# S5 in a hybrid mixer block: one operation for both scan directions, and a sum moved from VectorE to TensorE

## The chip, the cores and the metric

The kernel runs on one core of a Trainium2 chip. The metric is the time of one execution on the device in microseconds, the median of several runs. The engines are called as in the profile: PE is TensorE (matmuls), DVE is VectorE, ACT is ScalarE, POOL is GpSimd, SP is SyncE, which only issues transfers. ACT and POOL also issue transfers from their own queues. Each engine and each queue works through its instructions in the order written by the scheduler of the program.

## The reference

Two layers of a latent generator at batch 1: 512 latent tokens and 256 context tokens of 1024 channels. In each layer one input projection is split into four mixers, their outputs are put together and projected, and a SwiGLU follows. The change is in the fourth mixer, S5: 16 groups of 16 channels, 64 complex states per group, two directions. Cut to what matters here:

```python
ab_re, ab_im, z_re, z_im = s5_discretize(a_re[r], a_im[r], log_dt[r])   # (G, P), direction r
bb_re = z_re[..., None] * b_re - z_im[..., None] * b_im
bb_im = z_re[..., None] * b_im + z_im[..., None] * b_re
bu = einsum('gpc,blgc->blgp', bb, u)                   # complex input of the state
h_t = ab * h_{t-1} + bu_t                              # complex scan over tokens
y = einsum('gcp,blgp->blgc', c_re, h_re) - einsum('gcp,blgp->blgc', c_im, h_im)
y_total = u * d_skip + y(forward) + y(reversed)        # then gelu and a gated projection
```

The latent scan starts from the last context state of its direction.

## The kernel before

Activations lie with channels on partitions and tokens along columns. Large projections are made in three matmuls each from a high and a low part of weight and activation (`whi`, `wlo`, `ahl`, `alol` and so on), the parts split by ACT and DVE from weights that SP loads into three rotating tiles `wst` (`weights`, `piece`). The adaLN modulation of layer 0 (`mod`) loads its weights `in_wm` through the same tiles and multiplies into the PSUM ring `md`, which has one buffer.

**S5.** The 768 tokens (context, latent) are cut into 96 steps of 8. Per state the scan over the 96 steps is real: the rotation by the angle of the eigenvalue is taken out first and put back behind. So there are four parts:

- `s5_prep` (L1445): powers 0 to 8 of each eigenvalue and their products with the input coefficient, for all groups and both directions (32 columns), with real parts and imaginary parts on the two halves of the partitions. They land in `S` (tile `early` for layer 0, `S5S` for layer 1) at `S_X`, `S_N`, `S_Y`, `S_M`. The columns are ordered direction first, then group.
- `rotations` (L1512): cosine and sine of 96 multiples of an angle, as the complex product of 16 fine and 6 coarse ones (`R`, `R2`), for two groups at a time (`NG = 2`): `cmul` makes six DVE operations on 192 columns (tiles `cst`, `s5tq`), and ACT's queue writes each block of two groups to DRAM (`s5r`). There are 8 blocks.
- `s5_mats` (L1560): for each block and direction the input matrix `W` (8 steps by 16 channels) and the output matrix `oe` (9 steps by 16 channels, in tile `s5M`), each from two products and a difference. PE transposes `W`, ACT copies the transpose into `s5M`, PE makes the kernel inside one step (`Kf`), and ACT's queue writes it to DRAM eight times shifted (`s5k`).
- `s5_block` (L1642): SP loads the rotations (`s5rot`), the matrix `KT` from `s5k` and the input `U`. PE makes the state's input twice (`pv`), DVE multiplies by cosine and sine and adds (`gt`, `g2`), four scans run over the steps (line 1686, tile `g`), DVE multiplies again by the cosine (`gt`) and, with the halves of the partitions exchanged, by the sine (`sg`, in the profile `s5sg`), and adds both. `s5_y` (L1702) sums `KT` times `U` and `oe` times `gt` in PSUM, ring `md`, and ACT's queue writes the result to DRAM (`s5y`). `s5_out` reads it back (`s5fu`, `s5fy`).

For layer 0 (`run=True`) matrices and blocks are made together, in the first 300 us, beside the input projections and the Hyena filters (`hw`, `fs`, `flo`, `fo`, `win`, `ftab`, `F0l`). For layer 1 `prepare` (L1761) makes tables and matrices during layer 0's SwiGLU, writes them to DRAM, and `s5` loads them.

**What sets the order.** The program gives each part a priority (a lower number first) and a scheduler writes one order per engine by it, by the dependences and by its own running estimate of when an instruction could start. Layer 0's norms and first projections have 10000, `rotations` 9000, Hyena's context filters 36000, S5 40000, Hyena's latent filters 45000; projection matmuls get 300000 more (`bulk`), so that they fill the gaps of PE. A tile with `bufs=2` has two buffers, and its next user waits for the one before last.

Of the kernel before, what the change touches and what calls it, by code (L numbers as in the profile page):

```python
# [106 lines left out]
class Kern:  # L107
# [1337 lines left out]
    def s5_prep(self, i, S, p):  # L1445
# [30 lines left out]
        for q, x in enumerate((c, s_)):  # L1476
            for r in range(2):
                self.act(self.r8[64 * r:64 * r + 64, i, q], x[64 * r:64 * r + 64, 16 * r:16 * r + 16])
        X, N = S[:, 0:9], S[:, 9:18]
# [30 lines left out]
        self.cmul(S[:, self.S_Y:self.S_M], S[:, self.S_M:self.S_END], X[:, 0:8], N[:, 0:8], bc(zr, 8), bc(zi, 8), T)  # L1510

    def rotations(self, i, p):  # L1512


        R = p.tile([128, 44, 16], F32, name="rot")
        T = p.tile([128, 8, 16], F32, name="rotT")
        w = p.tile([128, 3, 16], F32, name="rotw")
        c, s_, t = w[:, 0], w[:, 1], w[:, 2]
        self.ts(w[:, 0:2], self.r8[:, i], 1.0)
        for at, n in ((0, 16), (32, 6)):  # L1520
            C, S = R[:, at:at + n], R[:, at + n:at + 2 * n]
# [16 lines left out]
        rd = self.dr.tile([16 // self.NG, 128, 2 * self.NG * 96], F32, name=f"s5r{i}")  # L1538
        for b in range(16 // self.NG):
            gs = slice(self.NG * b, self.NG * (b + 1))  # L1540
            cst = p.tile([128, 2, self.NG, 6, 16], F32, tag="cst", name="cst", bufs=2)
            tq = p.tile([128, self.NG, 6, 16], F32, name="s5tq")

            def fine(j):
                return R2[:, 16 * j:16 * j + 16, gs].rearrange("p b g -> p g b")[:, :, None, :].to_broadcast(
                    [128, self.NG, 6, 16])

            def coarse(j):
                return R2[:, 32 + 6 * j:38 + 6 * j, gs].rearrange("p a g -> p g a")[:, :, :, None].to_broadcast(
                    [128, self.NG, 6, 16])  # L1550
            self.cmul(cst[:, 0], cst[:, 1], coarse(0), coarse(1), fine(0), fine(1), tq)
            nc = self.nc
            nc.scalar.dma_start(rd[b], cst)
        return rd
# [5 lines left out]
    def s5_mats(self, i, p, S=None, run=False):  # L1560
# [12 lines left out]
        sh = [128, NG, 8, 16]  # L1573
        for b, g0 in enumerate(range(0, 16, NG)):
            M = p.tile([128, self.O_END], F32, tag="s5M", name="s5M", bufs=2)
            BC = p.tile([128, 6, NG, 16], F32, tag="s5BC", name="s5BC", bufs=2)
# [3 lines left out]
            ws = {}  # L1580
            for r in range(2):
                lg = slice(16 * r + g0, 16 * r + g0 + NG)

                def pw(at, n, rev):
                    v = S[:, at:at + n, lg]
                    if rev:
                        v = v[:, ::-1]
                    return v.rearrange("p t g -> p g t")[:, :, :, None].to_broadcast([128, NG, n, 16])

                def bc(q, n):  # L1590
                    return BC[:, q][:, :, None, :].to_broadcast([128, NG, n, 16])
                br, bi, cr, ci = bc(0, 8), bc(1, 8), bc(2 + r, 9), bc(4 + r, 9)

                Wt = p.tile(sh, F32, tag=f"W{r}", name="W", bufs=1 if run else 2)
                tmp = p.tile([128, NG, 9, 16], F32, tag="s5tmp", name="s5tmp")
                self.mul(Wt, pw(self.S_Y, 8, r == 0), br)
                self.mul(tmp[:, :, :8], pw(self.S_M, 8, r == 0), bi)
                self.sub(Wt, Wt, tmp[:, :, :8])
                ws[r] = Wt
                self.mul(oe[:, r], pw(self.S_X, 9, r == 1), cr)  # L1600
                self.mul(tmp, pw(self.S_N, 9, r == 1), ci)
                self.sub(oe[:, r], oe[:, r], tmp)
            W4 = self.pst()
            for g in range(NG):
                for r in range(2):
                    q = 128 * (NG * r + g)
                    nc.tensor.transpose(W4[:, q:q + 128], ws[r][:, g].rearrange("p t c -> p (t c)"), self.ident)
# [34 lines left out]
    def s5_block(self, i, b, p, M, kd, rd):  # L1642
# [8 lines left out]
        rot = p.tile([128, 2, 2, NG * 96], F32, tag="s5rot", name="s5rot", bufs=2)  # L1651
        for h in range(2):
            nc.sync.dma_start(rot[64 * h:64 * h + 64], rd[b].rearrange("(r n) x -> n r x", r=2))
        ct, st = rot[:, :, 0], rot[:, :, 1]
# [19 lines left out]
        def fl(t):  # L1674
            return t.rearrange("p r g b -> p r (g b)")
        self.mul(fl(gt), pv[0][:, :nn].rearrange("p (r x) -> p r x", r=2), ct)
        self.mul(fl(g2), pv[1][:, :nn].rearrange("p (r x) -> p r x", r=2), st)
        self.add(gt, gt, g2)
        for g in range(NG):
            for r in range(2):  # L1680
                lg = 16 * r + g0 + g
# [6 lines left out]
        sg = p.tile([128, 2, NG, 96], F32, tag="sg", name="s5sg")  # L1688
        self.mul(fl(gt), fl(g2), ct)
        self.stt(fl(sg)[0:64], fl(g2)[64:128], -1.0, st[64:128], ALU.mult, ALU.mult)  # L1690
        self.mul(fl(sg)[64:128], fl(g2)[0:64], st[0:64])
        self.add(gt, gt, sg)
        if i == 0:
            self.s5_y(i, b, p, KT, U, gt, oe, c0)
            return

        with self.at(self.tc.cur_priority + self.LAG):
            self.s5_y(i, b, p, KT, U, gt, oe, c0)
# [3 lines left out]
    def s5_y(self, i, b, p, KT, U, gt, oe, c0):  # L1702
# [321 lines left out]
def layout(inputs):  # L2024
# [93 lines left out]
```

## Time and profile before

| | us |
|---|---|
| median of three runs (1887.65 to 1890.61) | 1889.87 |
| the profiled execution | 1895.85 |
| its span, first to last instruction | 1894.1 |
| PE busy | 1761.3 |
| DVE busy | 1369.3 |
| ACT busy | 771.1 |
| POOL busy | 209.6 |

[...] Busy times are sums of what the profiler recorded for an engine's instructions, without double counting; the ends of matmuls are modelled. The span is divided between the engines very unevenly, so the stretches count more than the totals.

### The profile page before, as it was taken

To read this page: it belongs to the slowest core of one execution; us is meant where nothing else is said; L and a number is where in the kernel's file an instruction comes from. 1 tells how busy PE (TensorE), PEld (TensorE's weight loads), DVE (VectorE), ACT (ScalarE), POOL (GpSimd) and SP (SyncE) were. 2 spreads that over 40 slices of the span, in tenths; PEclk is the share of its full clock that TensorE was granted. 3 is DMA by queue.
4 is the path that set the end of the run, shared out by engine and by line. 5 is a ranking of instruction groups with operands and counts; after the bars stand their busy time and mean duration, and the time that the engine had idled before them with its cause. 6 is when DMAs were issued, how large, how long until landed. Compare 5 with 4: busy or idle time off the path is not lost.

```text
span 1894.1 us, 30868 instructions
## 1 busy us (share of the span) xinstructions
PE 1761.3 (93%) x11512; PEld 1539.6 (81%) x11512; DVE 1369.3 (72%) x3169; ACT 771.1 (41%) x1515; POOL 209.6 (11%) x273
## 2 busy tenths in 40 slices
PE   3789878898899999999999999999898889999997
PEld 1678767686789988888888899988776889899997
DVE  8788764677758899686675425689667797777776
ACT  4364234555326323321133223624575374344442
POOL 0201121223002000011123100201200010000000
PEclk9899979998899999999999999999999889999998
DMA  6657688765622335666654621665564323233331
GB/s 233 183 141 189 150 174 233 234 203 171 186 78 90 112 117 151 202 197 211 222 147 117 178 69 47 186 210 171 154 192 141 95 72 110 98 104 98 104 108 57
DMA packets 193098, 280.99 MB, mean 148 GB/s; under 512 B 51745, under 2 KB 127837, under 8 KB 192436
## 3 DMA queue, kind: packets, MB, share of 16 engines
q1 hardware_dynamic: 107188, 166.20, 29.0%
q10 hardware_dynamic: 55920, 64.72, 11.3%
q0 software_dynamic: 29840, 48.09, 9.4%
q8 instruction: 91, 1.49, 0.3%
q14 instruction: 59, 0.48, 0.1%
HBM read 235.00 MB, written 43.96 MB: 147 GB/s over the span
## 4 chain that ended last, share of the span: by engine, by line
PE 55%; DVE 12%; DMA 11%; issue 5%; ACT 4%; POOL 1%; ACTq 0%; SPq 0%; DVEq 0%; POOLq 0%
PE ps_mm L126 20%; PE ps_xb L126 12%; PE ps_xa L126 8%; PE ps_mm L487 6%; DMA mvw<-in_wmt_dram 5%; PE ps_md L126 4%; PE ps_xb L487 3%; PE ps_xa L487 1%; ACT L155 1%; DVE wlo L134 1%; DVE mvo L364 1%; DMA wst<-in_wi_dram 1%; DVE xl L152 1%; ACT E L155 1%; DMA wst<-in_wo_dram 1%
## 5 line engine op out<-in xcount | busy, mean ns | idle before, releaser
L155 ACT ACTIVATE whi<-wst 128x1024 fp32r<-128x1024 f32 (+3 forms) x206 | 179.8, 903 | 294.9 <-PE ps_mm L126 105.4
L134 DVE TENSOR_TENSOR wlo<-wst,whi 128x1024 fp32r<-128x1024 f32 (+3 forms) x206 | 213.1, 1050 | 71.0 <-ACT whi L155 69.9
L126 PE MATMUL ps_mm<-alol,whi 128*128 128x512 f32 (+1 forms) x528 | 199.5, 379 | 0.4 <-POOL alol L134 0.4
L126 PE MATMUL ps_mm<-ahl,whi 128*128 128x512 f32 (+1 forms) x528 | 197.6, 380 | 2.3 <-DVE BC L152 2.0
L126 PE MATMUL ps_mm<-ahl,wlo 128*128 128x512 f32 (+1 forms) x528 | 198.8, 377 | 0.0
L364 DVE SCALAR_TENSOR_TENSOR mvo<-mvw,crow 128x1024 f32<-128x1024 f32 x80 | 97.8, 1222 | 42.0 <-DMA mvw<-in_wmt_dram 40.7
L126 PE MATMUL ps_mm<-h,whi 128*128 128x512 f32 (+1 forms) x440 | 121.5, 358 | 2.4 <-DVE h L134 2.0
L126 PE MATMUL ps_mm<-ahc,whi 128*128 128x256 f32 x368 | 106.8, 294 | 12.3 <-ACT whi L155 8.3
L126 PEld LDWEIGHTS ps_mm<-ahl,whi 128*128 128x128 f32 x528 | 100.2, 192 | 19.9 <-issue 3.7
L126 PEld LDWEIGHTS ps_mm<-alol,whi 128*128 128x128 f32 x528 | 100.6, 190 | 19.3 <-issue 3.0
L126 PEld LDWEIGHTS ps_mm<-ahl,wlo 128*128 128x128 f32 x528 | 100.5, 190 | 16.8 <-issue 0.8
L126 PE MATMUL ps_mm<-aloc,whi 128*128 128x256 f32 x368 | 107.2, 292 | 1.6 <-DVE aloc L134 1.6
L126 PE MATMUL ps_mm<-ahc,wlo 128*128 128x256 f32 x368 | 106.1, 290 | 0.3 <-DVE wlo L134 0.3
L126 PE MATMUL ps_xb<-ahl,whi 128*128 128x512 f32 (+1 forms) x256 | 91.3, 361 | 5.6 <-ACT ahl L155 5.4
L126 PE MATMUL ps_xb<-alol,whi 128*128 128x512 f32 (+1 forms) x256 | 91.3, 359 | 0.5 <-DVE alol L134 0.3
L126 PE MATMUL ps_xb<-ahl,wlo 128*128 128x512 f32 (+1 forms) x256 | 90.8, 355 | 0.0
L126 PEld LDWEIGHTS ps_mm<-h,whi 128*128 128x128 f32 x440 | 75.7, 189 | 12.9 <-DVE h L134 2.5
L126 PEld LDWEIGHTS ps_mm<-ahc,whi 128*128 128x128 f32 x368 | 71.7, 197 | 15.8 <-ACT whi L155 8.5
L155 ACT ACTIVATE h<-sg 128x512 fp32r<-128x512 f32 (+1 forms) x70 | 37.3, 537 | 110.6 <-DVE sg L134 110.5
L126 PE MATMUL ps_xb<-h,whi 128*128 128x256 f32 x432 | 81.5, 284 | 0.0
L126 PE MATMUL ps_mm<-h,wlo 128*128 128x512 f32 (+1 forms) x220 | 78.9, 359 | 0.0
L155 ACT ACT_TABLE_LOAD x55 | 70.6, 1283 | 20.4 <-DMA vec<-in_vec_dram 3.6
(645 smaller groups left out, 5204.0 us busy)
## 6 DMA issues: line engine op xcount, KB each, us to landing
wst<-in_wu_dram SPq DMA_DIRECT2D x88, 512.0 KB
mvw<-in_wmt_dram POOLq DMA_DIRECT2D x56, 512.0 KB, 3.8
wst<-in_wi_dram SPq DMA_DIRECT2D x42, 512.0 KB
wst<-in_wm_dram SPq DMA_DIRECT2D x40, 512.0 KB
wst<-in_wd_dram SPq DMA_DIRECT2D x24, 384.0 KB
ftab<-in_c_ftL_dram POOLq DMA_DIRECT2D x32, 256.0 KB, 5.4
wst<-in_wd_dram SPq DMA_DIRECT2D x32, 256.0 KB
s5rot<-s5r SPq DMA_DIRECT2D x32, 192.0 KB
```

Source lines behind the costliest of these rows:

```text
L126: return self.nc.tensor.matmul(out, lhsT, rhs, start=start, stop=stop)
L134: return (eng or self.nc.vector).tensor_tensor(out, a, b, op=op)
L152: return self.nc.vector.scalar_tensor_tensor(out, a, s, b, op0=op0, op1=op1)
L155: return self.nc.scalar.activation(out, in_, func, bias=bias, scale=scale)
L364: self.nc.vector.scalar_tensor_tensor(o, st, 1.0, crow[:, q], op0=ALU.mult, op1=ALU.mult, accum_out=mv[:, c, q:q + 1])
L487: self.nc.tensor.matmul(ps, w[:, k], x[k], start=first and k + q == 0, stop=k + q == 5, skip_group_check=not first)
```

## The change

1. **Columns.** The 32 columns of the tables are ordered block, direction, group instead of direction, group; the host lays out `s5a` and `s5bc` so. A block's two directions lie side by side.
2. **Reversal once.** `s5_prep` makes the powers in a tile `F` (`s5F`), and eight ACT copies bring them to `S`, with the steps turned round for the direction that needs it. Before, each use read them turned round.
3. **Matrices.** `s5_mats` makes `W` and `oe` for both directions in one operation: six on 512 or 576 columns instead of twelve on 256 or 288.
4. **Rotations.** The fine table holds, side by side, (cos, sin) in one tile and (-sin, cos) in another; a table block is coarse cosine times the first plus coarse sine times the second: three operations on 384 columns. In DRAM and in `s5rot`, runs of 16 cosines and 16 sines alternate. ACT makes the four tiles in twelve copies.
5. **Layer 0 only.** ACT makes a second output matrix `os` from `oe`, with the partition halves exchanged and one of them negated, in a wider `s5M` (1920 columns instead of 1344; before the copies that part holds the temporary of `s5_mats`). The sine product `sg` is taken without exchange, in one operation, and is not added to `gt`; `s5_y` multiplies `gt` by `oe` and `sg` by `os` and sums in PSUM. `sg` has two buffers. Layer 1 keeps the old form.

```diff
-        self.cmul(S[:, self.S_Y:self.S_M], S[:, self.S_M:self.S_END], X[:, 0:8], N[:, 0:8], bc(zr, 8), bc(zi, 8), T)
+        self.cmul(F[:, self.S_Y:self.S_M], F[:, self.S_M:self.S_END], X[:, 0:8], N[:, 0:8], bc(zr, 8), bc(zi, 8), T)
+        for at, n, rev in ((self.S_X, 9, 1), (self.S_N, 9, 1), (self.S_Y, 8, 0), (self.S_M, 8, 0)):
+            for r in range(2):
+                t = F[:, at:at + n]
+                self.act(self.by_dir(S[:, at:at + n], r), self.by_dir(t[:, ::-1] if r == rev else t, r))
...
-        R2 = p.tile([128, 44, 16], F32, name="rot2")
-        self.act(R2[0:64], R[0:64])
-        for at, n in ((0, 16), (16, 16), (32, 6), (38, 6)):
-            self.act(R2[64:128, at:at + n], R[64:128, at:at + n][:, ::-1])
+        fine = [p.tile([128, 16, 2, 16], F32, name=f"rotf{j}") for j in range(2)]
+        coarse = [p.tile([128, 16, 6], F32, name=f"rotc{j}") for j in range(2)]
...
+            for j in range(2):
+                self.act(fine[j][hs, :, j], rows(0, 16))
+                self.act(fine[j][hs, :, 1 - j], rows(16, 16), scale=-1.0 if j else 1.0)
+                self.act(coarse[j][hs], rows(32 + 6 * j, 6))
...
-            self.cmul(cst[:, 0], cst[:, 1], coarse(0), coarse(1), fine(0), fine(1), tq)
+            for j, t in enumerate((cst, tq)):
+                self.mul(t, coarse[j][:, gs][:, :, :, None].to_broadcast(sh),
+                         fine[j][:, gs].rearrange("p g q b -> p g (q b)")[:, :, None, :].to_broadcast(sh))
+            self.add(cst, cst, tq)
...
-                self.mul(Wt, pw(self.S_Y, 8, r == 0), br)
-                self.mul(tmp[:, :, :8], pw(self.S_M, 8, r == 0), bi)
-                self.sub(Wt, Wt, tmp[:, :, :8])
-                ws[r] = Wt
-                self.mul(oe[:, r], pw(self.S_X, 9, r == 1), cr)
-                self.mul(tmp, pw(self.S_N, 9, r == 1), ci)
-                self.sub(oe[:, r], oe[:, r], tmp)
+            self.mul(Wt, pw(self.S_Y, 8), bc(0, 8))
+            self.mul(tmp[:, :, :8], pw(self.S_M, 8), bc(1, 8))
+            self.sub(Wt, Wt, tmp[:, :, :8])
+            self.mul(oe, pw(self.S_X, 9), bc(2, 9))
+            self.mul(tmp, pw(self.S_N, 9), bc(3, 9))
+            self.sub(oe, oe, tmp)
+            if run:
+
+                oe, os = [M[:, c:c + self.O_END - self.O_OE] for c in (self.O_OE, self.O_END)]
+                self.act(os[0:64], oe[64:128])
+                self.act(os[64:128], oe[0:64], scale=-1.0)
...
         self.mul(fl(gt), fl(g2), ct)
-        self.stt(fl(sg)[0:64], fl(g2)[64:128], -1.0, st[64:128], ALU.mult, ALU.mult)
-        self.mul(fl(sg)[64:128], fl(g2)[0:64], st[0:64])
-        self.add(gt, gt, sg)
         if i == 0:
-            self.s5_y(i, b, p, KT, U, gt, oe, c0)
+            self.mul(fl(sg), fl(g2), st)
+        else:
+            self.stt(fl(sg)[0:64], fl(g2)[64:128], -1.0, st[64:128], ALU.mult, ALU.mult)
+            self.mul(fl(sg)[64:128], fl(g2)[0:64], st[0:64])
+            self.add(gt, gt, sg)
...
+            for q, (oe, x) in enumerate(parts):
+                O = [oe[:, r, g, 1 - r:9 - r].rearrange("p t c -> p (t c)") for r in range(2)]
+                self.mm(o[:, f0:], O[0], x[:, 0, g, f0 - 1:95], False, False)
+                if need_c:
+                    self.mm(o[:, 0:31], O[1], x[:, 1, g, 65:96], False, False)
+                self.mm(o[:, 32:], O[1], x[:, 1, g, 1:65], False, q == len(parts) - 1)
```

**The order of the instructions.** It is written anew, and in layer 0's mixers it differs in most places; in layer 1 and in SwiGLU it is nearly the same. Three places count here. First DVE near layer 0's second last block (`g_2202` and `g_2172` are the tile of the four scans; `s5tmp`, `fo`, `hin` and `fr0l` belong to the next block's matrices, the Hyena filter and its convolution). Before:

```order
L134 TENSOR_TENSOR s5tmp<-early,s5BC 128x288
L134 TENSOR_TENSOR fo<-ps_xb,fe 128x256
L134 TENSOR_TENSOR fo<-fe,ps_xb 128x256
L1686 SCALAR_TENSOR_TENSOR g_2202<-dec_98,gt 128x96 x4
L134 TENSOR_TENSOR s5M<-s5M,s5tmp 128x288
L134 TENSOR_TENSOR gt<-g_2202,s5rot 128x384
L152 SCALAR_TENSOR_TENSOR s5sg<-g_2202,s5rot 64x384
L134 TENSOR_TENSOR s5sg<-g_2202,s5rot 64x384
L152 SCALAR_TENSOR_TENSOR hin<-ps_mm,vec,hin 128x511
L152 SCALAR_TENSOR_TENSOR hin<-ps_mm,vec,hin 128x255
L134 TENSOR_TENSOR gt<-gt,s5sg 128x384
```

And after the change:

```order
L134 TENSOR_TENSOR g_2172<-ps_xa,s5rot 128x384
L152 SCALAR_TENSOR_TENSOR frv<-ps_xb,vec 128x2
L149 TENSOR_SCALAR fr0l<-ps_xb 128x2
L134 TENSOR_TENSOR s5M<-early,s5BC 128x576
L134 TENSOR_TENSOR gt<-gt,g_2172 128x384
L757 RECIPROCAL fr0l<-fr0l 128x2
L134 TENSOR_TENSOR s5M<-s5M 128x576
L1705 SCALAR_TENSOR_TENSOR g_2172<-dec_98,gt 128x96 x4
L134 TENSOR_TENSOR gt<-g_2172,s5rot 128x384
L134 TENSOR_TENSOR s5sg<-g_2172,s5rot 128x384
```

The scans stand behind 545 rows of DVE before and 472 now; two half-height products and an addition have become one product.

Then PE at the last of layer 0's S5 blocks, where the output is summed (`ps_md`); `fh` and `w_1453` belong to the Hyena filter. Before:

```order
L126 MATMUL ps_xa<-s5U,s5M 128x96 x4
L126 MATMUL ps_xb<-w_1453,fh 128x256 x2
L126 MATMUL ps_md<-s5U,KT 128x96
L126 MATMUL ps_xb<-w_1453,fh 128x256 x2
L126 MATMUL ps_md<-gt,s5M 128x95
L126 MATMUL ps_md<-gt,s5M 128x31
L126 MATMUL ps_md<-gt,s5M 128x64
L126 MATMUL ps_md<-s5U,KT 128x96
L126 MATMUL ps_md<-gt,s5M 128x95
L126 MATMUL ps_md<-gt,s5M 128x31
L126 MATMUL ps_md<-gt,s5M 128x64
```

And after the change:

```order
L126 MATMUL ps_md<-gt,s5M 128x95
L126 MATMUL ps_md<-gt,s5M 128x31
L126 MATMUL ps_md<-gt,s5M 128x64
L126 MATMUL ps_md<-s5sg,s5M 128x95
L126 MATMUL ps_md<-s5sg,s5M 128x31
L126 MATMUL ps_md<-s5sg,s5M 128x64
L126 MATMUL ps_md<-s5U,KT 128x96
L126 MATMUL ps_md<-gt,s5M 128x95
L126 MATMUL ps_md<-gt,s5M 128x31
L126 MATMUL ps_md<-gt,s5M 128x64
L126 MATMUL ps_md<-s5sg,s5M 128x95
L126 MATMUL ps_md<-s5sg,s5M 128x31
```

Each row is a matmul that the chip runs as two instructions. Three rows on `s5sg` have come to each group's three on `gt`.

Last SP's queue behind the last loads of layer 0's S5 blocks (`glw`, `s5fu` and `s5fy` are the loads of `s5_out`, `win` and `F0l` the Hyena filter's). Before:

```order
L727 DMA win<-in_c_winL_dram 128x512 x2
L1658 DMA KT<-s5k_1632 128x1x128
L727 DMA win<-in_c_winL_dram 128x512 x2
L1658 DMA KT<-s5k_1632 128x1x128
L207 DMA wst<-in_wm_dram 128x1024
L207 DMA wst<-in_wi_dram 128x1024
L1729 DMA glw<-in_glu_dram 128x512
L1735 DMA s5fu<-s5u_427 128x8x32
L1737 DMA s5fy<-s5y_1633 128x8x32 x2
```

And after the change:

```order
L1677 DMA KT<-s5k_1627 128x1x128 x2
L785 DMA F0l<-fo 128x2x256 x4
L1753 DMA glw<-in_glu_dram 128x512
L727 DMA win<-in_c_winL_dram 128x512
L1759 DMA s5fu<-s5u_422 128x8x32
L1761 DMA s5fy<-s5y_1628 128x8x32
L727 DMA win<-in_c_winL_dram 128x512
L1761 DMA s5fy<-s5y_1628 128x8x32
L207 DMA wst<-in_wm_dram 128x1024
L207 DMA wst<-in_wi_dram 128x1024
```

The two weight loads stood ahead of S5's read-back and now stand behind its first part.

## Rows read from the trace of the kernel before

**Rows 1.** The page, busy times of each engine over the whole span.
```profile
PE 1761.3 (93%) x11512; PEld 1539.6 (81%) x11512; DVE 1369.3 (72%) x3169; ACT 771.1 (41%) x1515; POOL 209.6 (11%) x273
```

**Rows 2.** Busy us (count) by stretch of PE, PEld, DVE, ACT, POOL; clock; DMA share, GB/s.
```profile
45.00:85.00 40.00, 30.64 (x234) 24.16 (x226) 32.88 (x81) 16.20 (x32) 8.34 (x8) 0.91 0.50 160
100.00:260.00 160.00, 145.43 (x903) 120.95 (x903) 134.66 (x318) 69.23 (x144) 21.76 (x23) 0.94 0.65 165
150.00:200.00 50.00, 50.00 (x304) 41.21 (x304) 38.98 (x91) 18.32 (x43) 8.47 (x10) 1.00 0.78 202
220.00:300.00 80.00, 58.65 (x357) 47.17 (x356) 47.15 (x106) 24.27 (x51) 14.88 (x19) 0.79 0.85 182
280.00:290.00 10.00, 1.93 (x15) 1.67 (x14) 1.51 (x4) 3.70 (x7) 1.47 (x3) 0.83 1.50 273
700.00:850.00 150.00, 149.61 (x900) 128.23 (x899) 126.54 (x290) 45.21 (x98) 8.98 (x17) 1.00 0.59 182
```

**Rows 3.** Layer 0's decay scans between 100 and 300 us: count, ns, first and last start.
```profile
L1686 DVE TENSOR_TENSOR_SCAN g<-dec,gt x32: 323/330/1353, 121.4 to 257.1; 128x96 f32<-128x96 f32 x32
```

**Rows 4.** SyncE's queue in order of time: start us, us, queue, line, transfer.
```profile
257.02 0.59 SPq L1658 DMA_DIRECT2D KT<-s5k  x1
...
267.50 0.33 SPq L207 DMA_DIRECT2D wst<-in_wm_dram  x1
...
269.97 4.93 SPq L1737 DMA_DIRECT2D s5fy<-s5y  x2
```

**Rows 5.** SyncE queue waits, 200 to 300 us: total us, times, longest us.
```profile
SPq L1658 <- DMA s5k<-Kf: 18.4, 7, 5.3
SPq L207 <- PE ps_md L126: 14.7, 4, 9.9
```

**Rows 6.** Groups on VectorE, 0 to 700 us, the rotation tables: busy us, mean ns.
```profile
L134 DVE TENSOR_TENSOR cst<-rot 128x192 f32<-128x192 f32 x16 | 8.6, 579 | 3.3 <-DMA s5r<-cst 3.2
L134 DVE TENSOR_TENSOR s5tq<-rot 128x192 f32<-128x192 f32 x16 | 7.7, 484 | 0.2
L134 DVE TENSOR_TENSOR cst<-cst,s5tq 128x192 f32<-128x192 f32 x16 | 7.1, 446 | 0.3
```

**Rows 7.** The same view, the first layer's sine and cosine parts.
```profile
L152 DVE SCALAR_TENSOR_TENSOR s5sg<-g,s5rot 64x384 f32<-64x384 f32 x8 | 4.4, 554 | 0.1
L134 DVE TENSOR_TENSOR s5sg<-g,s5rot 64x384 f32<-64x384 f32 x8 | 4.4, 552 | 0.1
L134 DVE TENSOR_TENSOR gt<-gt,s5sg 128x384 f32<-128x384 f32 x8 | 4.4, 548 | 0.0
```

**Rows 8.** Groups on VectorE over the whole span, two widths.
```profile
L134 DVE TENSOR_TENSOR qp<-t,t 128x512 f32<-128x512 f32 x10 | 6.9, 687 | 0.2
L134 DVE TENSOR_TENSOR W<-S5S,s5BC 128x256 f32<-128x256 f32 x16 | 6.1, 414 | 0.0
```

**Rows 9.** Groups on ScalarE, 0 to 700 us, a copy of 512 columns.
```profile
L155 ACT ACTIVATE fhi<-fs 128x512 fp32r<-128x512 f32 x12 | 7.5, 629 | 22.4 <-DVE fs L134 18.8 <-DMA s5k<-Kf 2.3 <-DMA s5y<-ys 1.2
```

**Rows 10.** VectorE in order of time, two places: start us, us, operation.
```profile
213.54 0.68 DVE L134 TENSOR_TENSOR flo<-fs,fhi 128x512 fp32r<-128x512 f32 x1
214.14 0.55 DVE L134 TENSOR_TENSOR gt<-g,s5rot 128x384 f32<-128x384 f32 x1
...
243.09 0.45 DVE L134 TENSOR_TENSOR s5tmp<-early,s5BC 128x288 f32<-128x288 f32 x1
243.46 0.42 DVE L134 TENSOR_TENSOR fo<-ps_xb,fe 128x256 f32<-128x256 f32 x1
243.80 0.41 DVE L134 TENSOR_TENSOR fo<-fe,ps_xb 128x256 f32<-128x256 f32 x1
```

**Rows 11.** TensorE in order of time, one group's output sum.
```profile
238.36 0.78 PE L126 MATMUL ps_md<-gt,s5M 128*128 128x95 f32 x6
238.97 0.41 PE L126 MATMUL ps_md<-s5U,KT 128*128 128x96 f32 x2
```

**Rows 12.** Instructions on the tile gt alone, 100 to 300 us.
```profile
100.00:300.00 200.00, 14.43 (x96) 13.48 (x96) 27.97 (x64) 0.90 0.71 171
```

More of the change, by code (lines that the diff above doesn't have):

```diff
@@ new lines, in rotations, with rows @@
+        for h in range(2):
+            hs = slice(64 * h, 64 * h + 64)
+            def rows(at, n):
+                v = R[hs, at:at + n]
+                return (v[:, ::-1] if h else v).rearrange("p b g -> p g b")
+            for j in range(2):
+                self.act(fine[j][hs, :, j], rows(0, 16))
+                self.act(fine[j][hs, :, 1 - j], rows(16, 16), scale=-1.0 if j else 1.0)
+                self.act(coarse[j][hs], rows(32 + 6 * j, 6))
+        n = self.NG * 6
+        rd = self.dr.tile([16 // self.NG, 128, 32 * n], F32, name=f"s5r{i}")
@@ L1554, in rotations @@
+            self.add(cst, cst, tq)
+            self.nc.scalar.dma_start(rd[b], cst.rearrange("p g a x -> p (g a x)"))
         return rd
@@ L1572, in s5_mats @@
             md = self.dr.tile([128, 16 // NG, self.O_END], F32, name=f"s5m{i}")
-        sh = [128, NG, 8, 16]
         for b, g0 in enumerate(range(0, 16, NG)):
-            M = p.tile([128, self.O_END], F32, tag="s5M", name="s5M", bufs=2)
-            BC = p.tile([128, 6, NG, 16], F32, tag="s5BC", name="s5BC", bufs=2)
+            M = p.tile([128, self.O_END + (self.O_END - self.O_OE if run else 0)], F32, tag="s5M", name="s5M", bufs=2)
+            BC = p.tile([128, 4, 2 * NG, 16], F32, tag="s5BC", name="s5BC", bufs=2)
@@ new lines, in s5_mats, with pw, bc @@
+            oe = M[:, self.O_OE:self.O_END].rearrange("p (q t c) -> p q t c", q=2 * NG, t=9)
+            def pw(at, n):
+                v = S[:, at:at + n, 2 * NG * b:2 * NG * (b + 1)]
+                return v.rearrange("p t q -> p q t")[:, :, :, None].to_broadcast([128, 2 * NG, n, 16])
+            def bc(q, n):
+                return BC[:, q][:, :, None, :].to_broadcast([128, 2 * NG, n, 16])
+            Wt = p.tile([128, 2 * NG, 8, 16], F32, tag="W", name="W", bufs=1)
+            if run:
+                tmp = M[:, self.O_END:].rearrange("p (q t c) -> p q t c", q=2 * NG, t=9)
+            else:
+                tmp = p.tile([128, 2 * NG, 9, 16], F32, tag="s5tmp", name="s5tmp")
@@ new lines, in s5_mats @@
+            self.mul(Wt, pw(self.S_Y, 8), bc(0, 8))
[4 more added lines that the diff above has]
+            self.sub(oe, oe, tmp)
+            if run:
+                oe, os = [M[:, c:c + self.O_END - self.O_OE] for c in (self.O_OE, self.O_END)]
+                self.act(os[0:64], oe[64:128])
+                self.act(os[64:128], oe[0:64], scale=-1.0)
@@ L1650, in s5_block @@
         oe = M[:, self.O_OE:self.O_END].rearrange("p (r g t c) -> p r g t c", r=2, g=NG, t=9)
-        rot = p.tile([128, 2, 2, NG * 96], F32, tag="s5rot", name="s5rot", bufs=2)
+        rot = p.tile([128, 2, NG * 192], F32, tag="s5rot", name="s5rot", bufs=2)
         for h in range(2):
             nc.sync.dma_start(rot[64 * h:64 * h + 64], rd[b].rearrange("(r n) x -> n r x", r=2))
-        ct, st = rot[:, :, 0], rot[:, :, 1]
+        ct, st = [rot.rearrange("p r (y q b) -> p r y q b", q=2, b=16)[:, :, :, q] for q in range(2)]
         KT = p.tile([128, NG, 128], F32, tag="KT", name="KT", bufs=2)
@@ L1674, in fl @@
         def fl(t):
-            return t.rearrange("p r g b -> p r (g b)")
-        self.mul(fl(gt), pv[0][:, :nn].rearrange("p (r x) -> p r x", r=2), ct)
-        self.mul(fl(g2), pv[1][:, :nn].rearrange("p (r x) -> p r x", r=2), st)
+            return t.rearrange("p r g (a b) -> p r (g a) b", b=16)
+        for t, v, x in ((gt, pv[0], ct), (g2, pv[1], st)):
+            self.mul(fl(t), v[:, :nn].rearrange("p (r y b) -> p r y b", r=2, b=16), x)
         self.add(gt, gt, g2)
```

71 lines of the change are left out of this document (29 added, 42 removed).

## The prediction

> **What bounds the kernel now.** I read first the page's line of busy times: TensorE (PE) 1761.3 of 1894.1 us, VectorE (DVE) 1369.3 [rows 1]. On average PE bounds, but the change touches only some stages, so the next view is each engine's busy time by stretches [rows 2]. From 700 to 850 us, where layer 1's tables and matrices are made, PE is busy 149.61 of 150: a faster DVE finds nobody waiting there. From 45 to 85 us, where layer 0's rotation tables are made, DVE has 32.88 of 40 and PE only 30.64. From 100 to 260, where layer 0's eight S5 blocks run, both are nearly full: DVE 134.66 and PE 145.43 of 160 (shares 0.84 and 0.91) [rows 2].
>
> Where does that last stretch end? The eight groups of scans run from 121.4 to 257.1 us [rows 3]. In SyncE's queue (SP) the last load of S5's kernel matrix KT is issued at 257.02; then nothing until the weight load at 267.50, and behind it the S5 output is read back [rows 4]. The weight load waited for a PE matmul of the one-buffer PSUM ring that S5's output also uses; the longest of these waits is 9.9 us [rows 5]. [...] So the end of layer 0's S5 blocks decides when the projections go on, and its time is worth something.
>
> **The change part by part.** All prices are of the profiled execution (1895.85 us, span 1894.1); the median of the three runs, 1889.87, lies 5.98 below it, and I carry the difference over to the median.
>
> *Rotation tables, layer 0.* Before, six DVE operations on 192 columns for each of 8 blocks: 8.6 + 7.7 + 7.1 = 23.4 us [rows 6]. After, three on 384 columns. The nearest row, two tensors on 384 columns, has 4.4 us for 8 [rows 7], so 24 cost 13.2: 10.2 us saved. The new operands repeat one table value over 32 columns and read the other in runs of 32. Runs of 16 cost nothing: the product W<-S5S,s5BC, which reads so, takes 414 ns [rows 8], plain sums fo<-fe of the same 256 columns 0.41 and 0.42 us [rows 10]. If instead the wide products kept the price per column of the old ones (two of 484 ns for one wide one), 16 would cost 15.5 and 8 sums 4.4: 3.5 saved. Below zero I see no reason, since no column is added. Of the 10.2 I count half, 5.1 us, because PE is idle for only part of that stretch [rows 2]. ScalarE (ACT) makes twelve short copies ahead of the tables instead of five. It is busy 16.20 of 40 there [rows 2] and hides them; if not, seven at the 0.63 us of a 128 x 512 copy [rows 9] are 4.4 us at most, which the half not counted covers.
>
> *Matrices, layer 0.* Twelve operations per block become six of twice the width. A 256-column one is followed by the next after 0.34 us (243.46 to 243.80), a 512-column one after 0.60 (213.54 to 214.14) [rows 10]: 0.08 saved per pair. A 288-column one takes 0.37 to the next [rows 10], and by the same slope, 0.26 us for 256 more columns, a 576-column one takes 0.67: 0.07 saved. Three pairs of each, 8 blocks: (0.24 + 0.21) x 8 = 3.6. By mean durations (414 twice against the 687 of a 512-column sum [rows 8]) a pair saves 0.14, so 6.7 us for all 48 pairs is the upper end. [...] The starts in the trace disagree [rows 10]: the next operation begins before the former has ended. I go by the starts.
>
> *The first layer's parts.* Per block one full-height product replaces two half-height ones, and an addition goes: 4.4 + 4.4 + 4.4 - 4.4 = 8.8 us [rows 7]. In exchange the output sum takes six more matmul instructions for each of 16 groups, 96 in all. Six of the same kind start at 238.36 and the next follows at 238.97, 0.61 us [rows 11], so 16 x 0.61 = 9.8 us of PE. The upper bound is the union of all 96 present ones, waits between them included: 14.43 us [rows 12].
>
> *ACT in each layer-0 block* gets two 64 x 576 copies for the swapped matrix. A 128 x 512 copy has 0.63 us [rows 9], so some 0.7 each and 11 us in all. ACT is busy 69.23 of 160 in the S5 stretch [rows 2], so I price them at zero. They wait for the block's last DVE difference, and behind them stand that block's two PSUM evictions and the KT rows. The matrices are made one block ahead, with two buffers, and that hides it; without that cover each block loses 1.4 us, 11 us in all. The eight copies that turn the powers round are once per layer.
>
> *Layer 1* saves as much in tables and matrices, under a full PE: zero. Its S5 blocks keep their number of DVE operations; the rotation rows are now read in runs of 16, which [rows 8] prices at nothing.
>
> *The sum.* DVE removed in the S5 stretch, 3.6 + 8.8 = 12.4 us, is worth the share of time that DVE is busy there: 12.4 x 0.84 = 10.4. PE added is worth PE's share: 9.8 x 0.91 = 8.9. Sum: -5.1 - 10.4 + 8.9 = -6.6 us. 1895.85 - 6.6 = 1889.3 for a profiled execution, 1889.87 - 6.6 = 1883.3, say **1883.5 us** for the median. What is late next: the weight loads, whose place in SP's queue moves (below).
>
> **The rivals.**
>
> *PE has room after all (faster).* If the 96 instructions fall into gaps in which PE waits, they cost nothing, and the sum is -5.1 - 10.4 = -15.5: 1874.4 us. For it: from 220 to 300 PE lacks 21.35 us of 80 [rows 2]. Against it: from 150 to 200 PE is busy 50.00 of 50. [...]
>
> *SP's queue gives it back (no change).* Before, the two weight loads stand ahead of the read-back of S5's output; after, behind it. The read-back is issued from 269.97 for 4.93 us, so its end, 274.90, is 7.4 us behind the first weight load at 267.50 [rows 4]. If PE starves for these, -6.6 + 7.4 = +0.8: 1890.7 us. For it: PE is busy 1.93 of 10 from 280 to 290 [rows 2], when the first of these weights have just come. Against it: S5's end itself moves forward, and fewer projections have been used up by then.
>
> *PE takes DVE's place (slower).* Place: the S5 stretch, 114 to 264 us. If the blocks move at the pace of their loads and not of DVE (KT waited 18.4 us for its rows between 200 and 300 [rows 5]), DVE's 12.4 us are worth little while the 96 instructions cost their upper price, 14.4 x 0.91 = 13.1. It decides when DVE's saving is worth less than a third: at a sixth, -5.1 - 2.1 + 13.1 = +5.9, 1895.8 us. For it: PE at 50.00 of 50 from 150 to 200 [rows 2]. Against it: DVE's 134.66 of 160 [rows 2], and that projections that PE puts off can fill the later gaps.
>
> *The wide operations are not cheaper* enters through its bound: 3.5 instead of 10.2 saved in tables, half counted, moves the sum by 3.3 us, to 1886.8.
>
> **How the numbers follow.** Forecast 0.37, PE has room 0.19, SP's queue 0.23, PE takes over 0.21. A difference under 0.2% (3.8 us) is about what a measurement of this kernel cannot tell from no change. The forecast and the first rival are faster: 0.56; the second same: 0.23; the third slower: 0.21. Range: upward to the third rival, 1896; downward to the first with DVE's saving worth all of itself and all of the tables (-10.2 - 12.4 = -22.6, 1867.3): 1868.
>
> **What would show it.** DVE busy some 36 us lower in all, about 23 of it before 260 us; PE busy up to 10 us higher; the last group of scans starting at about 242 instead of 257; the weight loads of 267.50 earlier by more than 5 us; wide table operations near 0.55 us. Wrong would be: the last scans at the same time (the third rival); scans earlier but the weight loads not (the second); a difference that appears after 600 us, where I see none.

## The result and the profile after

The changed kernel takes 1917.36 us (median of 4 runs, 1908.94 to 1921.54), the kernel before 1890.24 beside it: ratio 1.0121, 95% interval 1.0095 to 1.0147, so slower by 1.2%, where 1883.5 was forecast and 1896 was the upper end of the range. The profiled execution took 1908.94 (span 1907.1), the fastest of the four; it shows 13 us of the loss, not all 27 of the medians. Ratios, here and below, are the recorded ones; they can differ a little from the quotient of the two medians (here 1.0143).

The page's busy times, the stretches of [rows 2], then the scans and the tile gt of [rows 3, 12]:

```profile
PE 1770.2 (93%) x11608; PEld 1551.5 (81%) x11608; DVE 1340.4 (70%) x3009; ACT 796.5 (42%) x1564; POOL 211.2 (11%) x273
```
```profile
45.00:85.00 40.00, 31.33 (x245) 25.20 (x246) 30.21 (x72) 20.91 (x44) 11.17 (x12) 0.97 0.70 203
100.00:260.00 160.00, 150.94 (x1032) 128.44 (x1030) 121.80 (x264) 75.68 (x155) 25.43 (x25) 0.98 0.69 177
220.00:300.00 80.00, 71.25 (x426) 57.85 (x425) 37.08 (x75) 30.23 (x54) 16.09 (x21) 0.87 0.84 202
280.00:290.00 10.00, 10.00 (x65) 7.48 (x64) 2.30 (x5) 2.83 (x5) 2.67 (x4) 0.99 1.03 178
700.00:850.00 150.00, 149.85 (x909) 129.35 (x908) 119.81 (x250) 49.48 (x107) 7.38 (x14) 1.00 0.55 177
```
```profile
L1705 DVE TENSOR_TENSOR_SCAN g<-dec,gt x32: 321/333/358, 115.2 to 229.8; 128x96 f32<-128x96 f32 x32
100.00:300.00 200.00, 13.12 (x96) 12.37 (x96) 22.07 (x56) 0.94 0.72 182
```

Up to 300 us nearly all went as hoped or better: DVE does less, PE's hole at 280 is gone, the last scan starts 27 us earlier (257.1 to 229.8). The 96 new matmuls, on the tile s5sg, are busy 13.33 us (9.8 were priced, 14.4 at most). The first 300 us, before and after:

```profile
0.00:300.00 300.00, 231.99 (x1464) 188.23 (x1465) 231.30 (x687) 124.36 (x253) 42.15 (x51) 0.91 0.69 181
```
```profile
0.00:300.00 300.00, 244.33 (x1623) 202.47 (x1624) 216.87 (x610) 147.86 (x297) 46.79 (x53) 0.95 0.71 191
```

PE stands still 55.7 us instead of 68.0. The weight load of 267.50 [rows 4] is issued at 250.64, indeed behind a part of the read-back of S5's output, as SyncE's queue shows:

```profile
248.35 0.63 SPq L1761 DMA_DIRECT2D s5fy<-s5y  x1
250.07 0.52 SPq L1761 DMA_DIRECT2D s5fy<-s5y  x1
250.64 0.66 SPq L207 DMA_DIRECT2D wst<-in_wm_dram  x1
```

The loss comes later. The output projection of layer 0 reads what the four mixers (S5, SSD, hyena, retention) have written to DRAM. Its first load of the context's residual, xo, is issued at 500.60 before and 519.93 after; I divide both spans there, and call the place the cut (columns as in [rows 2]). Before:

```profile
0.00:500.60 500.60, 415.34 (x2750) 339.50 (x2751) 378.27 (x1022) 226.59 (x477) 86.61 (x99) 0.91 0.68 190
500.60:1894.10 1393.50, 1345.94 (x8763) 1200.12 (x8761) 991.07 (x2148) 544.54 (x1039) 122.97 (x174) 0.98 0.44 134
```

After:

```profile
0.00:519.90 519.90, 427.28 (x2840) 352.20 (x2841) 356.30 (x934) 245.41 (x510) 88.30 (x99) 0.91 0.64 184
519.90:1907.10 1387.20, 1342.95 (x8769) 1199.33 (x8768) 984.06 (x2076) 551.05 (x1055) 122.90 (x174) 0.98 0.43 134
```

Up to the cut PE is busy 11.9 us longer (9.8 were priced for the 96 matmuls) and stands still 92.6 us instead of 85.3. Together that is the 19.3 us; 6.3 come back behind the cut. Since PE's idle time was 12.3 us less by 300 us, it grew by 19.7 between there and the cut, from 17.3 to 36.9. DVE's work up to the cut fell by 22.0 us, about the 22.6 that were priced for layer 0 (10.2 + 3.6 + 8.8), and PE's idle time did not fall with it.

The 11.9 us cannot be put down to the 96 matmuls from these rows. The kernel before with one priority number changed (run before_flt, below) has nearly the same matmuls up to its cut, 2748, and is busy 426.73 us with them, 11.4 longer, at a clock of 0.89 against 0.91:

```profile
0.00:521.60 521.60, 426.73 (x2748) 347.30 (x2749) 376.09 (x1022) 229.76 (x478) 86.06 (x99) 0.89 0.64 183
```

Who is late at the cut? The mixers' writes on ACT's queue, before (hx is the hyena, sin the SSD, ry the retention of the context; the l or c behind yd0 is for latents or context):

```profile
328.68 0.33 ACTq L281 DMA_DIRECT2D yd0l<-s5yo  x1
348.40 0.33 ACTq L281 DMA_DIRECT2D yd0c<-s5yo  x1
...
481.59 0.33 ACTq L281 DMA_DIRECT2D yd0l<-hx  x1
489.01 0.98 ACTq L281 DMA_DIRECT2D yd0l<-sin  x2
...
496.99 0.33 ACTq L281 DMA_DIRECT2D yd0c<-ry  x1
```

and after:

```profile
503.69 3.51 ACTq L281 DMA_DIRECT2D yd0l<-hx  x2
508.25 0.98 ACTq L281 DMA_DIRECT2D yd0l<-sin  x2
509.33 0.93 ACTq L281 DMA_DIRECT2D yd0c<-ry  x2
```

S5's last output was written at 348.40 before the change, 150 us ahead of the cut. The projection's loads of it, on SyncE's queue, began at 449.25 with the latents' half, which had lain there since 328.68 (hyena and SSD write theirs from 478 us on):

```profile
449.25 0.90 SPq L1914 DMA_DIRECT2D yl<-yd0l  x2
...
462.79 2.44 SPq L1914 DMA_DIRECT2D yl<-yd0c  x4
```

S5 was not the late branch; hyena, SSD and retention are, and each ends 12 to 25 us later than before. The last of these writes moved by 12.8 us. The other 6.5 of the 19.3 lie between it and the cut, where PE now stands 5.5 us for ACT's part of the projection's input (yhl, in the second view below). What PE waited for, 240 to 530 us (total us, times, longest), before and then after:

```profile
PE ps_mm L126 <- ACT whi L155: 8.3, 1, 8.3
PE ps_xb L126 <- ACT sE L155: 5.5, 1, 5.5
...
PE ps_md L126 <- ACT mrow L155: 0.7, 1, 0.7
```
```profile
PE ps_xb L126 <- DVE ztl L134: 7.6, 2, 6.6
PE ps_md L126 <- ACT mrow L155: 6.1, 4, 4.1
PE ps_mm L126 <- ACT yhl L155: 5.5, 1, 5.5
```

The mrow wait can be followed on ACT in order of time (start us, us). In the modulation chunks of layer 0 a row is copied out of PSUM (mrow), and PE turns it. Here the copy stands behind three reloads of ACT's function table, 1.28 us each: a Silu (rg) and the SSD's exponentials (E) alternate, and one reload stands at each turn between them (a fourth follows behind the copy):

```profile
449.60 1.28 ACT L155 ACT_TABLE_LOAD   x1
450.90 0.60 ACT L155 ACTIVATE rg<-ps_mm 128x512 f32<-128x512 f32 x1
451.51 1.28 ACT L155 ACT_TABLE_LOAD   x1
...
452.81 0.98 ACT L155 ACTIVATE E<-E,sbias 128x128 f32<-128x128 f32 x3
453.81 1.28 ACT L155 ACT_TABLE_LOAD   x1
455.11 0.38 ACT L155 ACTIVATE rg<-ps_mm 128x256 f32<-128x256 f32 x1
455.39 0.38 ACT L155 ACTIVATE mrow<-ps_md 128x256 f32<-128x256 f32 x1
```

Four small matmul instructions on that row stand next in PE's order, and nothing that stands behind them starts before them: PE stands for 4.05 us (the bracket is idle time before, and its releaser):

```profile
455.82 1.02 PE L126 MATMUL ps_md<-const,mrow 128*128 128x2 f32 x4 [4.05 <-ACT mrow L155]
458.34 1.09 PE L126 MATMUL ps_xa<-vd,Bt 128*64 128x256 f32 x2 [1.51 <-DVE vd L134]
```

### The profile page after: what moved, and what is told of

Read it like the earlier page. It is cut to its first block, busy times and chain, and to the rows that moved or that the text cites. A ratio compares the mean times of both kernels' runs of the same rounds, so it can differ in the third digit from the quotient of the medians.

```text
span 1907.1 us, 30959 instructions
## 1 busy us (share of the span) xinstructions
PE 1770.2 (93%) x11608; PEld 1551.5 (81%) x11608; DVE 1340.4 (70%) x3009; ACT 796.5 (42%) x1564; POOL 211.2 (11%) x273
## 4 chain that ended last, share of the span: by engine, by line
PE 56%; DMA 7%; DVE 7%; issue 4%; ACT 2%; POOL 0%; ACTq 0%; SPq 0%; DVEq 0%; POOLq 0%
PE ps_mm L126 20%; PE ps_xb L126 14%; PE ps_xa L126 8%; PE ps_mm L487 6%; DMA mvw<-in_wmt_dram 4%; PE ps_md L126 3%; PE ps_xb L487 3%; PE ps_xa L487 1%; DVE wlo L134 1%; DVE mvo L364 1%; ACT L155 1%; DVE xl L152 1%; DMA wst<-in_wo_dram 1%; DVE gt L134 0%; DMA wst<-in_wd_dram 0%
```

## The experiments

The two parts of the change were run apart, and each version under several orders. "Matmuls alone" is point 5 of the change: 96 matmuls and 16 ACT copies more, and 8.8 us of DVE's work less. "Wide alone" is the rest. An order is what the scheduler makes of the program; one priority number changed leaves the work as it is and moves the mixers against each other. (The rows with mrow also move one copy from ACT to DVE, as told below.) The numbers are ratios to the kernel before, with 95% intervals.

| order | before | wide alone | matmuls alone | changed |
|---|---|---|---|---|
| as it was | 1 | 1.0049 [1.003, 1.0068] | 1.0061 [1.0044, 1.0078] | 1.0121 [1.0095, 1.0147] |
| hyl3 | 1.0038 [1.0023, 1.0053] | 1.0123 [1.0099, 1.0146] | 1.0112 [1.0081, 1.0142] | 1.0127 [1.0106, 1.0148] |
| flt | 1.0151 [1.0124, 1.0178] | 1.0033 [1.0014, 1.0051] | 1.0115 [1.0092, 1.0139] | 1.0069 [1.0046, 1.0092] |
| mrow | 1.0149 [1.0123, 1.0175] | 0.9997 [0.9987, 1.0008] | | 1.0044 [1.0027, 1.0062] |
| hyl3, mrow | | 0.9996 [0.9978, 1.0013] | | 1.0024 [1.001, 1.0039] |
| flt, mrow | | 0.9996 [0.9978, 1.0014] | | |
| flt, hyl3, mrow | | 1.0027 [1.0014, 1.004] | | |
| hyl3, ret3, mrow | | 0.995 [0.9932, 0.9968] | | |

**The parts apart.** Wide operations alone, against the changed kernel:

```diff
-                self.act(os[0:64], oe[64:128])
-                self.act(os[64:128], oe[0:64], scale=-1.0)
...
-            self.s5_y(i, b, p, KT, U, [(oe, gt), (os, sg)], c0)
+            self.s5_y(i, b, p, KT, U, [(oe, gt)], c0)
```

> The changed kernel without the taking apart in layer 0: the wide rotation tables and matrices stay, the parts are combined on DVE as before, and the 96 extra matmuls and the 16 extra ACT copies are gone. Theory ORDER (the loss comes from the order that the scheduler makes of the mixers: S5 and the SSD go first, the hyena of the latents becomes the last thing that the output projection waits for): its hyena of the latents also stands near the end of DVE's order, so little or nothing is gained, 1895 to 1915 us, and the last write of the hyena's latents lands well after 481.6, where it was before. Theory PE (the 96 extra matmuls, 9.8 us, and their clock make the loss): 1870 to 1882 us, since the DVE savings of about 13 us stay and the matmuls are gone.

The matmuls alone, against the kernel before:

```diff
+                self.act(es[0:64], eo[64:128])
+                self.act(es[64:128], eo[0:64], scale=-1.0)
...
-            self.s5_y(i, b, p, KT, U, gt, oe, c0)
+            self.s5_y(i, b, p, KT, U, [(oe, gt), (os, sg)], c0)
```

> The kernel before with only the taking apart in layer 0 (96 more matmuls, 16 more ACT copies, 24 DVE operations fewer on 128x384 or half of it); tables and matrices as before. Theory ORDER: what it costs depends on where the hyena of the latents ends; in its order that stands some 40 DVE instructions before the outputs, between the two kernels, so 1888 to 1905 us. Theory PE: the matmuls add what they take, 9.8 us, less nothing, and the lower clock more: 1900 to 1912 us.

Measured 1904.34 and 1909.79 us beside 1897.54. The first is in ORDER's range and the second in PE's, above ORDER's. Theory PE falls for the first: a kernel with less DVE work and the same PE work got slower. In its trace the last scan starts at 242.8, S5's writes come 13 to 15 us earlier, yet the hyena ends at 495 and the SSD at 502.

**The hyena of the latents first (hyl3).** In both kernels:

```diff
-                with self.flow("xb", chunk((5, 0)[i])):
+                with self.flow("xb", chunk((3, 0)[i])):
```

> The changed kernel with one number changed: the hyena of the latents of layer 0 is put ahead of the SSD of the latents (chunk 3 in place of 5; the SSD's is 4). Every operation stays. Theory ORDER: its last write comes at or before 490 us instead of 506.9, the output projection starts 10 to 20 us earlier, 1888 to 1902 us. Theory PE: the same work, so 1910 to 1920 us as the changed kernel.

> The kernel before with the same number changed. Both theories: there the hyena's latents were done at 481.6, some 15 us before the last input of the output projection (the retention of the context, 496.99), so this gains nothing: 1886 to 1896 us. If it gains as much as the changed kernel does by it, the number is worth something by itself and ORDER is not shown by the other run.

1922.11 and 1902.99 us: the repair fails, and the second lies above the 1886 to 1896 that both theories gave. The hyena did end earlier in the changed kernel (501 instead of 507), but the SSD then ended at 522. That the hyena of the latents alone is to blame is gone; and the kernel before lost 0.4% by a number that changes no work.

**The latents' filters ahead of S5 (flt).**

```diff
-                    with self.flow("xb", 36000 if s is sc else 45000):
+                    with self.flow("xb", 36000 if s is sc else 39000):
```

> The changed kernel without layer 0's taking apart, and with the latents' hyena filters put ahead of S5 (priority 39000 in place of 45000; S5 has 40000). Theory HYENA (the path to the output projection is filters of the latents, hyena of the context, hyena of the latents; S5's own end has some 150 us to spare; in the kernel with wide operations alone the filters' last write came at 322 us against 306 before, and the rest of the mixers 13 to 20 us early): the last filter write comes at 300 us or earlier, the hyena of the latents ends 15 to 20 us earlier than in that kernel, and the whole takes 1880 to 1892 us, under the kernel before. Theory PATHLESS (any new order costs 5 to 15 us, since the order of before was the best of many, and no single branch is to blame): 1898 to 1912 us, wherever the filters end.

> The changed kernel whole, with the latents' hyena filters ahead of S5 as in the run beside it. Theory HYENA: the filters end some 10 us earlier than 303, the hyena of the latents well before 500 instead of at 507, and the time is that of the other run plus what 96 matmuls take on PE (9.8 us): 1890 to 1902 us. Theory PATHLESS: 1905 to 1925 us, as the changed kernel.

> The kernel before with the same one number changed, as a control. S5's scans will end later than 257. Theory HYENA: the filters end a little earlier than 306, S5's later end costs nothing, 1885 to 1896 us. Theory S5 (S5's chain sets when the mixers end, as the prediction had it): the time grows by what the last scans are late, 1896 to 1910 us. Theory PATHLESS: 1896 to 1912 us, without regard to the scans.

1899.35, 1906.44 and 1918.96 us beside 1893.91. With wide operations alone the filters ended at 293 instead of 322 and the hyena of the latents began 33 us earlier, but it still ended at 499: theory HYENA falls. The control is the telling one: S5's last scans start only 4 us later (261.4), and the kernel before is 25 us slower. Theory S5 allowed at most what the scans are late; 1918.96 lies above the ranges of all three theories.

**The table of orders completed.**

> Wide tables and matrices alone, with the hyena of the latents ahead of the SSD of the latents. With split_hyl3 and split_flt it completes a table of four versions (before, wide alone, split alone, changed) by three orders (as it was, hyena of the latents first, filters first). Theory DRAW (each edit of the program makes the scheduler deal a new order of the mixers, the deals differ by some 30 us in idle and low-clock time of PE, and the kernel before held a good one; the wide operations save DVE time that no deal waits for, the 96 matmuls add what they take): mean of wide over the three orders within 5 us of the mean of before over the same orders, so this run anywhere in 1885 to 1915 us. Theory ADD (each part has its own cost or gain, order aside): wide alone costs 0.3 to 0.5% in every order, so this run is 0.3 to 0.5% over before with the same order, 1908 to 1914 us.

> Layer 0's taking apart alone, with the hyena of the latents ahead. Theory DRAW: the mean of split over the three orders is 8 to 14 us over the mean of before over the same orders, since PE's work grows by 9.8 us in each; this run anywhere in 1895 to 1930 us. Theory ADD: 0.6% over before with this order, 1911 to 1918 us.

> Layer 0's taking apart alone, with the latents' filters ahead of S5. Theory DRAW: anywhere in 1895 to 1930 us, the mean over the three orders as in the run beside it. Theory ADD: 0.6% over before with this order, 1925 to 1935 us.

1919.07, 1916.53 and 1917.68 us. The first lies above the ranges of both theories, the second in both, the third in DRAW's alone. Theory ADD falls: wide alone costs 0.85% over before in the order hyl3 and gains 1.18% in flt. Over the first three rows of the table the columns have the means 1.0063, 1.0068, 1.0096 and 1.0106. So the wide operations make no difference in the mean there, and the kernel before was 0.63% better than the mean of its own three orders. The matmuls alone are 0.33% (6 us) over before; 8 to 14 had been expected of them.

**The modulation row copied by DVE (mrow).**

```diff
-            self.act(r, ps[:, :256])
+            self.nc.vector.tensor_copy(r, ps[:, :256])
```

> The changed kernel with the copy of the modulation row out of PSUM (mrow, 12 times in layer 0's mixers) on DVE instead of ACT. In the changed kernel PE stood for 4.05 us at 451.8 behind this copy, which stood on ACT behind four reloads of its function table (1.28 us each), and PE then ran at half clock from 458 to 470. Theory MROW (this block and the low clock behind it are what the changed order lost): PE's waits for mrow fall from 6.1 us to under 1, the time falls by 8 to 15 us to 1902 to 1910 us. Theory DRAW: the wait goes, but another takes its place with the new order, 1905 to 1925 us.

1902.97 us, in MROW's range and below DRAW's. The wait for the copy fell from 6.1 to 0.5 us. To see whether that was one more lucky order, the same line in four others:

> The kernel before with the modulation row copied by DVE instead of ACT. PE waited 0.7 us for that copy there. Theory MROW (gain = the wait that goes, and the low clock behind it): nothing to gain, within 0.3% of before, 1886 to 1897 us. Theory DRAW (a new order, no mechanism): like the two other orders tried with this kernel, 0.4 to 1.5% slower, 1900 to 1920 us.

> Wide operations alone (no extra matmuls) with the modulation row copied by DVE. PE waited 4.3 us for the copy in the kernel with wide operations alone (1904 us). Theory MROW: 5 to 10 us less, 1892 to 1900 us, at or near the kernel before. Theory DRAW: 1892 to 1920 us with no preference, the middle at 1905.

> The changed kernel with the hyena of the latents ahead (1922 us as it stood, PE's wait for the copy 2.4 us) and the row copied by DVE. Theory MROW: 3 to 6 us less, 1914 to 1920 us. Theory DRAW: 1900 to 1925 us.

> Wide operations alone, the latents' filters ahead of S5 (1899 us as it stood, the wait 4.8 us, 4.3 of it in one piece at 444 after which PE stood at half clock from 460 to 490), and the row copied by DVE. Theory MROW: 8 to 15 us less, 1884 to 1892 us, at or under the kernel before: the version that would beat both. Theory DRAW: 1892 to 1920 us.

1922.62, 1893.28, 1900.03 and 1895.26 us. With the wide operations the edit gained in every pair, also in the one completed below: 0.77 and 1.03% in the changed kernel, 0.52, 0.37 and 1.27% with wide alone. The size doesn't follow the measured wait (2.4 us gave 1.03%, 4.8 us 0.37%), so MROW holds in its sign only: three of the four times are outside its ranges, while three are inside DRAW's and the fourth, 1922.62, just above. In the kernel before the edit costs 1.5%, where MROW expected no change and DRAW a loss of 0.4 to 1.5%. There PE waits for DVE's copy (view of PE's waits, 240 to 540 us), and the scans start 7 to 8 us later:

```profile
PE ps_md L126 <- DVE mrow L344: 5.2, 3, 3.6
```
```profile
L1686 DVE TENSOR_TENSOR_SCAN g<-dec,gt x32: 322/332/1353, 128.0 to 265.4; 128x96 f32<-128x96 f32 x32
```

So wide alone is 1.5% faster than before when both have the edit, in the one order in which both were run. That DVE's saved time is the reason is not shown: the fastest version below waits for DVE's copy nearly as long (240 to 530 us):

```profile
PE ps_md L126 <- DVE mrow L344: 3.8, 3, 1.6
```

**Candidates.** The retention of the context was the last branch in wide_mrow, so its priority was raised too in the third run:

```diff
-                    with self.flow("mm", chunk(6)):
+                    with self.flow("mm", chunk(3)):
```

> Wide operations alone, the modulation row copied by DVE, and the hyena of the latents ahead of the SSD of the latents. In wide_mrow the SSD of the latents was done at 472 and the hyena of the latents at 499, the last but one. Theory PE (the 96 matmuls cost what they take in the same order): 5 to 10 us under after_hyl3_mrow (1900 us), 1890 to 1895 us. Theory DRAW: 1885 to 1920 us.

> The same with the latents' filters ahead of S5 too, so that the hyena's chain starts some 20 to 30 us earlier. Theory MIXERS (the end is set by the latest of four branches, and a balanced end saves time): 1882 to 1892 us. Theory DRAW: 1885 to 1920 us.

> As wide_hyl3_mrow, with the retention of the context (the last of wide_mrow, 501) ahead of the SSD of the latents too. Theory MIXERS: 1882 to 1892 us. Theory DRAW: 1885 to 1920 us.

1891.68, 1899.20 and 1885.30 us beside 1894.27. The last one beats both kernels: ratio 0.995 (0.9932 to 0.9968). It is the best of eight versions of wide alone; the kernel before was never run in this order, so the 0.5% are not a measure of the wide operations. Hyena, SSD and retention end at 489, 485 and 492 us, and PE stands still for 76.9 us up to its cut, against 85.3 before. The second shows that this is no rule: it moves one branch more and is slower.

```profile
0.00:497.80 497.80, 420.95 (x2764) 340.69 (x2766) 373.01 (x979) 228.48 (x477) 85.84 (x99) 0.91 0.67 191
497.80:1882.70 1384.90, 1339.26 (x8751) 1197.43 (x8750) 981.03 (x2067) 548.50 (x1050) 123.09 (x174) 0.98 0.44 135
```

Point 5, the matmuls with the DVE work that they replace, can now be priced over all eight pairs of the table that share a row: +0.72, +0.04, +0.36, +0.47 and +0.28% on top of wide alone, +0.61, +0.74 and -0.36% on top of before, a mean of 0.36% or 6.8 us, with a 95% interval of 0.9 to 12.7 us if the pairs are taken as independent. For the wide operations the seven pairs give +0.49, +0.85, -1.18, -1.52 and, with the matmuls in both, +0.60, +0.15, -0.46%: a mean of -0.15% (-2.9 us), with an interval of -1.0 to +0.7% (-19 to +13 us).

## Why the prediction was wrong

**The step that failed** is the end of its first part: "So the end of layer 0's S5 blocks decides when the projections go on, and its time is worth something." The projections did go on earlier. But the output projection then waits for the latest of the other three mixers, and S5's output had lain there for 120 us when its first load was issued, and for 150 at the cut. By this step the sum took -10.4 us for DVE's saving in the S5 stretch, and it took -5.1 for the tables ahead of it. What the runs show in its place: 12.3 us less idle time of PE by 300 us, 19.7 more from there to the cut, and a total slower by 1.2%.

Over all twenty profiled executions, the last write of hyena, SSD or retention lies between 491 and 522 us, the span between 1882.7 and 1921.2, and the two go together (correlation 0.93). Behind the cut the span always has 1385 to 1395 us left. S5's last write is at least 148 us ahead of the last of the others in each. This shows where time is won and lost; being a correlation, it does not show what delays the late mixers.

The pairs do not settle what the saving is worth. The sum gave the wide operations -8.1 us (-5.1, and 3.6 x 0.84 = 3.0 for the matrices); the interval above holds -8.1 as well as zero.

**The local marks were right.** DVE is 28.9 us lower in all (36 forecast), 18.0 of it before 260 us (23 forecast), and PE 8.9 higher (up to 10). The last scans start 27 us earlier (15 forecast), the weight loads 17. The three rotation operations on 384 columns take 14.5 us where 13.2 were priced [rows 7]; first their groups, then two of them by tile (shortest, median and longest in ns):

```profile
L134 DVE TENSOR_TENSOR cst<-rotc,rotf 128x384 f32<-128x384 f32 x8 | 5.2, 666 | 2.0 <-DMA s5r<-cst 1.3 <-ACT rotc L155 0.7
L134 DVE TENSOR_TENSOR s5tq<-rotc,rotf 128x384 f32<-128x384 f32 x8 | 4.9, 606 | 0.1
L134 DVE TENSOR_TENSOR cst<-cst,s5tq 128x384 f32<-128x384 f32 x8 | 4.4, 552 | 0.1
```
```profile
L134 DVE TENSOR_TENSOR cst<-rotc,rotf x8: 545/549/1478, 47.7 to 71.0; 128x384 f32<-128x384 f32 x8
L134 DVE TENSOR_TENSOR s5tq<-rotc,rotf x8: 546/554/981, 48.7 to 69.8; 128x384 f32<-128x384 f32 x8
```

So "runs of 16 cost nothing" held. The means of 666 and 606 ns come from long single instructions, up to 1478 and 981 ns; the medians, 549 and 554, are those of the plain sum (552 in the mean). The products on s5rot, which is now read in runs of 16, take 550 to 555 ns in the mean; before, 541 to 554.

**The matmuls** were +8.9 in the sum. The 6.8 us of the runs are for all of point 5, which the sum priced at +1.5: 8.9 less the 7.4 (8.8 x 0.84) that it gave the DVE work in the same point. The interval of 0.9 to 12.7 holds both. PE's busy time, 8.9 us higher in all, fits the term; what the 96 matmuls cost in time is not shown apart.

**The rivals.** "PE takes DVE's place" named the right side and a time (1895.8) far too low; its mark, the last scans at the same time, is absent. "SP's queue gives it back" saw the weight loads fall behind the read-back, and they did, but 17 us earlier than before. That the order of all that follows would be made anew was counted as a moved queue only. It is probably the larger part: of the 1.21% the mean of point 5 explains 0.36; the rest, some 0.85%, is of the size of what one priority number does to the kernel before without any change of work (0.4 and 1.5%). That this rest is the order is a remainder, not a measurement, since no run held the order fixed while the work changed.

**What the profile had shown.** One view would have told: the DMAs that write S5's result (328.68 for the latents, 348.40 for the context) beside the first load of the projection that reads it (449.25). I looked at who waits near S5's end and not at who waits for S5's result.

## What to carry to other kernels

Before pricing time saved on a branch, find the instruction that reads the branch's result and how long the result has lain there by then. In a program whose order a scheduler makes, compare parts over several orders of both versions: one priority number moved this kernel by up to 1.5%, more than either part of the change does in the mean.

## What was not expected of the hardware

The granted clock fell at small stops. From 450 to 460 us after the change PE is busy 3.73 of 10 (the stop above, 451.77 to 455.82) and the clock is 0.72, in the next 10 us 0.60; from 460 to 500 it is 0.67 where before had 0.74:

```profile
450.00:460.00 10.00, 3.73 (x21) 2.48 (x20) 2.87 (x8) 9.54 (x17) 1.34 (x4) 0.72 0.36 121
460.00:470.00 10.00, 10.00 (x63) 7.54 (x64) 9.07 (x17) 1.92 (x5) 4.55 (x4) 0.60 0.45 146
```

The clock is told as a share of the full one, and these are means of stretches at 1.00 and at 0.50: in windows of 0.25 and 0.5 us it reads 1.00 up to 454.25, 0.50 from 454.50 to 467.50 and 1.00 from 468.00 to 474.50. The kernel before falls too, in nearly the same place, from 0.86 to 0.50 (by such windows 0.50 from 457.25 to 470.75; PE had stood 1.08 us before 455.69 and 0.68 us before 457.01):

```profile
450.00:460.00 10.00, 8.20 (x45) 6.12 (x44) 9.23 (x21) 7.51 (x18) 2.33 (x3) 0.86 0.52 171
460.00:470.00 10.00, 8.93 (x65) 5.93 (x64) 9.68 (x25) 2.05 (x5) 3.52 (x8) 0.50 0.68 212
```

Up to the cut the mean is 0.91 in both; from 300 us to the cut it is 0.92 before and 0.87 after. What makes the clock fall, and how much of the loss is the clock's, no run shows. While the clock is low PE can still read as fully busy (10.00 of 10 at 0.60), so a busy share has to be read with the clock beside it.
